# A one-core hybrid layer: another order of block sums, five raw buffers, the residual summed in HBM, transposes by full-width steps and transfers, six pairs by block sums

## The chip, the cores and the metric

The kernel runs on one core of one Trainium2 chip. Its time is device microseconds (us) of one execution, from launch to end. TensorE multiplies matrices and writes into PSUM (eight banks of 128 x 512 fp32); VectorE (DVE), ScalarE (ACT) and GpSimd (POOL) work element by element on SBUF; SyncE (SP) issues most of the transfers between HBM and SBUF, POOL a few.

## The reference

One transformer layer on 256 tokens of 2048 features, all in fp32. `h = rms_norm(x)`; one projection `h @ w_in` gives the inputs of 8 heads of attention (one block of 256 tokens, so the block selection has nothing to choose), of 4 heads of retention, and three gates. Then

```
merged = sigmoid(gate_a) * (oa @ w_o_attn) + sigmoid(gate_r) * (orr @ w_o_ret)
x  = x + merged @ w_out
h2 = rms_norm(x)
g, u = split(h2 @ w_ffn_in, 2)          # 2 x 5632 columns
return x + (silu(g) * u) @ w_ffn_out
```

All weights are read from HBM once, some 300 MB.

## The kernel before

Tokens are two blocks of 128 (`NB`), features are tiles of 128 (`kt`). Each product is `x^T` (features on partitions, stationary) times a weight tile of 128 x 512 (moving), summed over the features in a PSUM bank for each token block. For fp32 precision both operands are split in two fp32r parts, hi and lo, and a product is three matmuls: hi x hi, hi x lo, lo x hi (`mm3`, L97). A weight tile is split by ScalarE (hi, a copy that rounds, L91) and VectorE (lo, a subtraction, L92).

The work is a list of groups. A plain group (`plain`, L130) takes two feature tiles of one block of 512 columns: one split of 128 x 1024 and twelve matmuls. Eight of them make a column block; its evacuation (`ev_...`) follows the last one. The lists stand in the order of the stages: projection, output of attention and retention, `w_out`, then the feed-forward stage. Each turn of the loop at L765 issues loads for up to eight groups ahead (SP, three buffers `raw` of four tiles each), the split of group g, the matmuls of group g - 3, and the jobs due then (`later`, `run_jobs`). A scheduler then orders each engine's instructions by dependency, so neighbours can change places.

The feed-forward stage has eleven pairs j: 512 columns of g and the same of u. The hidden block `silu(g) * u` of each pair must be turned (features on partitions) before it is multiplied by `w_ffn_out`. The pairs come in parts of 3, 3, 3, 2; the output product of a part (`ev_fo`, L719) is done in the next part and added to x1 in SBUF by VectorE (L724), written out at the last part. Pairs in `PLAIN` are two plain column blocks, 192 matmuls. The others go through `strassen` (L183): sums of blocks of the weights (L231, L235, L236, on VectorE) and of x1 (`sum_forms`, made once) give the 2 x 2 blocks in seven products in place of eight: 168 matmuls, and seven more block adds at the evacuation (`ev_gu`, L696). `mixed` deals the groups of block sums evenly among the plain ones.

A turn of a tile (`transposed`, L381): 16 VectorE transposes of 32 partitions x 256 columns, then the hi and lo split. It is used for the query, key and retention inputs, and for the retention output, merged, x1 and hidden tiles (23 of the last four kinds). Buffers: `pair()` (five of 128 x 2 x 512), `unit()` (14 of 128 x 2048), PSUM tags `pm` and `sd` with four banks each.

Of the kernel before, what the change touches and what calls it, by code (L numbers as in the profile page):

```python
# [32 lines left out]
PLAIN = (0, 2, 4, 6, 8, 9)  # L33
# [8 lines left out]
def hybrid_layer_kernel(ctx, tc, xt, x, w_in, w_oa, w_or, w_out, qg, kg, gm, gf, w_fi, w_fo, out):  # L42
# [15 lines left out]

    nc = tc.nc
# [5 lines left out]
    sp = ctx.enter_context(tc.tile_pool(name="sp", bufs=1))  # L65
    att_scope = ExitStack()
# [60 lines left out]
    def rows(w, kts, a, ln):  # L127
        return w[kts[0] * P:(kts[0] + len(kts)) * P, a:a + ln].rearrange("(k p) n -> p k n", p=P)

    def plain(w, cols, kts, lhs, evac, before=None):  # L130
# [6 lines left out]
        def load(i):  # L137
# [38 lines left out]
        while j < len(kts):  # L176

            n = 1 if begin and j < FIRST else SPLIT_KT
            out_groups.append((lambda i=j - j % LOAD_KT: load(i), lambda j=j, n=n: split_(j, n), lambda j=j, n=n: mm(j, n)))
            j += n  # L180
        return out_groups

    def strassen(w, ca, cb, evac):  # L183
# [12 lines left out]
        def first_load(i):  # L196
# [3 lines left out]
            for n in range(2):  # L200
                nc.sync.dma_start(t[:, 2 * n:2 * n + 2, :], rows(w, [k1(4 * i + 2 * n), 0], ca, NC))
# [16 lines left out]
        def load(kk):  # L218
# [3 lines left out]
            for slots, c in ((slice(0, 4, 3), ca), (slice(1, 3), cb)):  # L222
                r = k1(kk) * P
                nc.sync.dma_start(t[:, slots, :], w[r:r + 3 * P, c:c + NC].rearrange("(k p) n -> p k n", p=P)[:, 0:3:2, :])

        def split_(kk, g):
# [154 lines left out]
    def transposed(d, tok, hi, lo, scale=None, sums=None):  # L381
# [192 lines left out]
    def ev_gr(h):  # L574
        def f(pm):
# [9 lines left out]
            transposed(2, y, hi[:, k, :], lo[:, k, :])  # L585
# [13 lines left out]
    def ev_o(n, which):  # L599
        def f(pm):  # L600
# [3 lines left out]
            if which == "r":  # L604
# [7 lines left out]
                transposed(0 if n == 3 else 2, t, hi[:, k, :], lo[:, k, :])  # L612
# [11 lines left out]
    def before_out():  # L624
        for i in range(2):
            x1[i] = unit(F32, (P, NB, 2 * NC))
            nc.sync.dma_start(x1[i], x[:, i * 2 * NC:(i + 1) * 2 * NC].rearrange("(b p) n -> p b n", p=P))

    def x1_cols(n):
        return x1[n // 2][:, :, n % 2 * NC:(n % 2 + 1) * NC]  # L630

    def ev_out(n):
        def f(pm):
            xc = x1_cols(n)
            t = pair()
            for b in range(NB):
                nc.vector.tensor_tensor(xc[:, b, :], pm[b], xc[:, b, :], op=ALU.add)
                nc.scalar.activation(t[:, b, :], xc[:, b, :], AF.Square, accum_out=ss2[:, b, n:n + 1])
            if n % 2 == 0:
                x1T[n // 2] = [unit(shape=(P, 8, S)) for _ in range(2)]  # L640
            hi, lo = x1T[n // 2]
            k = slice(n % 2 * 4, n % 2 * 4 + 4)
            if n % 2 == 0:
                sT[n // 2] = [unit(shape=(P, 2, 4, 2, P)) for _ in range(2)]
            transposed(0 if n == 3 else 2, xc, hi[:, k, :], lo[:, k, :], [g_ffn[:, n * 4 + j:n * 4 + j + 1] for j in range(4)],
                       sums=[t[:, n % 2] for t in sT[n // 2]])
# [23 lines left out]
    extra = []  # L670
# [147 lines left out]
```

## Time and profile before

| | |
|---|---|
| median of three runs | 1587.07 us (1586.04 to 1587.26) |
| the profiled execution | 1589.53 us, its span 1587.8 us |
| granted TensorE clock, mean | 0.988 |
| busy: TensorE, VectorE, ScalarE, POOL | 1540.5, 1244.1, 787.1, 22.8 us |
| matmuls | 6717 |
| transfers | 309.45 MB, 195 GB/s mean |

The span is the time between the first and the last instruction of the profiled execution; about 1.7 us lie around it. A matmul's row is its own duration, pipelined with the next: the step from one to the next is shorter. An engine's idle time matters only where the engine that sets the end waits for it. In the windows below 0 to 757 us reaches to the evacuation of the first column block of the `w_out` product, 828 to 967, 967 to 1190, 1190 to 1384.5 and 1384.5 to 1541 us the four parts of the feed-forward stage (cut at the evacuation of the last hidden block or output column of a part), with the last output product behind them.

### The profile page before, as it was taken

The numbers are of one execution on the slowest core, as the hardware profiler recorded it, in microseconds if no ns is written. First come the engines' busy times: TensorE is split into PE (matmuls) and PEld (weight loads), VectorE is DVE, ScalarE is ACT, GpSimd is POOL, SyncE is SP. The second block draws the span as 40 slices with busy tenths as digits, with TensorE's granted clock in tenths as the row PEclk, the third lists the DMA queues.
The fourth block names the chain that finished last, engine by engine and source line by source line (L and its number), as shares of the span: only waits on it lengthen the run. The fifth ranks groups of instructions, "written<-read, shape, count | busy, mean of one in ns | idle before, by whom it ended". The sixth has DMA issues, their size and how long they took to land.

```text
span 1587.8 us, 17802 instructions
## 1 busy us (share of the span) xinstructions
PE 1540.5 (97%) x6717; PEld 1251.0 (79%) x6717; DVE 1244.1 (78%) x1667; ACT 787.1 (50%) x904; POOL 22.8 (1%) x28
## 2 busy tenths in 40 slices
PE   9999999999999999999999897998999999999998
PEld 6788888888888888888887685676777887877787
DVE  7989877778666565657998979799898878788884
ACT  7465554545553444444465454553554544454442
POOL 1102000000000000000000000000000000000000
PEclk9999999999999999999999998998999999999999
DMA  9455555555565565575555564565666565665563
GB/s 346 161 183 179 174 177 186 185 174 183 178 207 186 189 197 197 186 258 176 198 167 198 180 209 153 192 206 164 209 211 229 192 214 194 205 211 179 194 237 133
DMA packets 163989, 309.45 MB, mean 195 GB/s; under 512 B 6176, under 2 KB 23104, under 8 KB 163648
## 3 DMA queue, kind: packets, MB, share of 16 engines
q1 hardware_dynamic: 163776, 308.31, 58.1%
q8 instruction: 52, 0.85, 0.2%
q14 instruction: 33, 0.27, 0.0%
q0 software_dynamic: 128, 0.02, 0.0%
HBM read 306.20 MB, written 2.10 MB: 194 GB/s over the span
## 4 chain that ended last, share of the span: by engine, by line
PE 64%; DVE 22%; DMA 6%; issue 4%; ACT 3%; SPq 0%; ACTq 0%; DVEq 0%
PE pm L100 20%; PE pm L101 20%; PE pm L99 20%; DVE wlo L92 11%; DVE e L410 6%; DMA raw<-in_w_fi 5%; ACT whi L91 2%; DVE raw L231 1%; PE sd L100 1%; PE sd L101 1%; PE sd L99 1%; DMA raw<-in_w_fo 1%; DVE u L92 1%; DVE raw L235 1%; DVE raw L236 1%
## 5 line engine op out<-in xcount | busy, mean ns | idle before, releaser
L91 ACT ACTIVATE whi<-raw 128x1024 fp32r<-128x1024 f32 (+1 forms) x614 | 637.3, 1054 | 631.8 <-PE pm L101 417.1
L92 DVE TENSOR_TENSOR wlo<-raw,whi 128x1024 fp32r<-128x1024 f32 (+1 forms) x614 | 739.6, 1219 | 268.8 <-ACT whi L91 262.7
L100 PE MATMUL pm<-wlo,u 128*128 128x512 f32 x1912 | 752.8, 394 | 19.4 <-DVE wlo L92 19.2
L99 PE MATMUL pm<-whi,u 128*128 128x512 f32 x1912 | 747.7, 393 | 13.7 <-ACT whi L91 8.1
L101 PE MATMUL pm<-whi,u 128*128 128x512 f32 x1912 | 749.0, 392 | 0.3 <-DVE u L92 0.3
L100 PEld LDWEIGHTS pm<-wlo,u 128*128 128x128 f32 x1912 | 361.6, 189 | 108.3 <-DVE wlo L92 34.1
L99 PEld LDWEIGHTS pm<-whi,u 128*128 128x128 f32 x1912 | 360.7, 189 | 96.6 <-ACT whi L91 15.6
L101 PEld LDWEIGHTS pm<-whi,u 128*128 128x128 f32 x1912 | 361.8, 189 | 75.8 <-DVE u L92 0.7
L410 DVE STREAM_TRANSPOSE e<-e 32x256 f32<-32x256 f32 x432 | 188.3, 436 | 11.0 <-ACT e L520 3.9
L99 PE MATMUL sd<-whi,u 128*128 128x512 f32 x160 | 62.4, 399 | 5.6 <-ACT whi L91 5.6
L100 PE MATMUL sd<-wlo,u 128*128 128x512 f32 x160 | 64.3, 402 | 1.5 <-DVE wlo L92 1.5
L231 DVE TENSOR_TENSOR raw<-raw 128x1024 f32<-128x1024 f32 x40 | 48.9, 1222 | 20.5 <-DMA raw<-in_w_fi 20.4
L101 PE MATMUL sd<-whi,u 128*128 128x512 f32 x160 | 63.5, 397 | 0.0
L91 ACT ACTIVATE u<-e 128x512 fp32r<-128x512 f32 (+1 forms) x56 | 34.5, 654 | 57.3 <-DVE e L410 55.6
L99 PEld LDWEIGHTS sd<-whi,u 128*128 128x128 f32 x160 | 30.3, 191 | 14.7 <-ACT whi L91 8.8
L92 DVE TENSOR_TENSOR u<-e,u 128x512 fp32r<-128x512 f32 (+1 forms) x56 | 39.5, 728 | 0.5 <-ACT u L91 0.5
L100 PE MATMUL pm<-wlo,h 128*128 128x512 f32 x96 | 37.7, 392 | 1.4 <-DVE wlo L92 1.3
L100 PEld LDWEIGHTS sd<-wlo,u 128*128 128x128 f32 x160 | 30.7, 192 | 10.2 <-DVE wlo L92 3.9
L101 PE MATMUL pm<-whi,h 128*128 128x512 f32 x96 | 37.4, 390 | 0.0
L99 PE MATMUL pm<-whi,h 128*128 128x512 f32 x96 | 37.0, 391 | 0.1
L101 PEld LDWEIGHTS sd<-whi,u 128*128 128x128 f32 x160 | 30.8, 192 | 6.3
L410 DVE STREAM_TRANSPOSE e<-u 32x256 f32<-32x256 f32 x64 | 27.9, 436 | 1.3
(142 smaller groups left out, 549.2 us busy)
## 6 DMA issues: line engine op xcount, KB each, us to landing
raw<-in_w_in SPq DMA_DIRECT2D x84, 1024.0 KB, 5.0
raw<-in_w_fi SPq DMA_DIRECT2D x100, 512.0 KB, 4.5
raw<-in_w_fi SPq DMA_DIRECT2D x48, 1024.0 KB, 5.1
raw<-in_w_fo SPq DMA_DIRECT2D x44, 1024.0 KB, 5.1
raw<-in_w_in SPq DMA_DIRECT2D x38, 512.0 KB, 4.3
raw<-in_w_or SPq DMA_DIRECT2D x16, 1024.0 KB, 5.0
raw<-in_w_out SPq DMA_DIRECT2D x16, 1024.0 KB, 5.0
raw<-in_w_oa SPq DMA_DIRECT2D x8, 1024.0 KB, 5.0
```

The source lines that it names most:

```text
L91: nc.scalar.activation(hi, src, AF.Copy)
L92: nc.vector.tensor_tensor(lo, src, hi, op=ALU.subtract)
L99: nc.tensor.matmul(o, lh, rh, start=start, stop=False)
L100: nc.tensor.matmul(o, lh, rl, start=False, stop=False)
L101: nc.tensor.matmul(o, ll, rh, start=False, stop=stop)
L231: nc.vector.tensor_tensor(t[:, 0:2, :], t[:, 0:3:2, :], t[:, 1:2, :].to_broadcast([P, 2, NC]), op=ALU.add)
L235: nc.vector.tensor_tensor(t[:, 0, :], t[:, 0, :], t[:, 2, :], op=ALU.add)
L236: nc.vector.tensor_tensor(t[:, 1, :], t[:, 0, :], t[:, 3, :], op=ALU.add)
L410: nc.vector.transpose(o[:, :, :, q, :], i[:, :, :, f * 32:(f + 1) * 32])
```

## The change

- `PLAIN` loses pair 8: six pairs by block sums, five plain.
- In `split_` the second and third weight sums (L245, L246 after) are made in slots 2 and 3, right behind the first operand's split; before they stood behind the second operand's, in slots 0 and 1.
- In the feed-forward stage five buffers hold raw weights (three `raw`, two `raw2` in the space that attention's constants and two hidden blocks had), and loads are issued 14 groups ahead, not 8.
- 23 tiles are turned by `moved`: two VectorE transposes of 128 partitions x 512 columns (32 x 32 blocks each), four transfers of 32 partitions each into a scratch tile in HBM, one transfer back that puts the 32-blocks in their place. They are issued by POOL, and for the last column of the merged and of the x1 tiles by SP. The hi and lo split then stands four plain groups behind (two for SP's).
- x is loaded by column into `pair()` buffers, x1 is stored to `out` at once, and each output product is copied by ScalarE and added to `out` in HBM by an accumulating transfer from POOL, 32 of 128 x 512.
- The evacuation of a pair by block sums is cut in four steps due at different groups; times of `later` count a plain group as two and a group of block sums as one.

```diff
-PLAIN = (0, 2, 4, 6, 8, 9)
+PLAIN = (0, 2, 4, 6, 9)
...
+        if extra and len(raws) % 5 > 2:
+            raws[key] = extra[0].tile([P, LOAD_KT, NC], F32, tag="raw2", bufs=2, name=nm("raw"))
...
                 split(hi, lo, t[:, 2:4, :])
+                nc.vector.tensor_tensor(t[:, 2, :], t[:, 0, :], t[:, 2, :], op=ALU.add)
+                nc.vector.tensor_tensor(t[:, 3, :], t[:, 2, :], t[:, 3, :], op=ALU.add)
             elif g == 1:
                 split(hi, lo, t[:, 0:2, :])
-                nc.vector.tensor_tensor(t[:, 0, :], t[:, 0, :], t[:, 2, :], op=ALU.add)
-                nc.vector.tensor_tensor(t[:, 1, :], t[:, 0, :], t[:, 3, :], op=ALU.add)
             else:
-                split(hi, lo, t[:, 0:2, :])
+                split(hi, lo, t[:, 2:4, :])
...
+    def moved(d, tok, hi, lo, gains=None, sums=None, tr=None):
+        tr = pair() if tr is None else tr
+        raw = pair().rearrange("p b c -> p (b c)").rearrange("p (q b k t) -> p q b k t", q=4, b=NB, t=32)
+        later(d, moved_rows, tok, tr, raw, nc.gpsimd if d else nc.sync)
+        later(d + 4 if d else 2, moved_split, raw, hi, lo, gains, sums)
+
+    def moved_rows(tok, tr, raw, queue):
...
+        for b in range(NB):
+            nc.vector.transpose(o[:, b], i[:, b])
+        d = dr.tile([4, P, 2 * P], F32, tag="d", bufs=4, name=nm("d"))
+        for q in range(4):
+            queue.dma_start(d[q].rearrange("(g j) x -> j g x", j=32),
+                            tr[q * 32:(q + 1) * 32].rearrange("j (g x) -> j g x", g=4))
+        queue.dma_start(raw.rearrange("p q b k t -> p q (b k t)"), d.rearrange("q p x -> p q x"))
...
     def ev_out(n):
-            xc = x1_cols(n)
+            xc = x1.pop(n)
...
+            nc.sync.dma_start(out[:, n * NC:(n + 1) * NC].rearrange("(b p) n -> p b n", p=P), xc)
...
     def hidden(j, t):
-        if j % 3 == 2:
-            hid[j] = extra[0].tile([P, 2, 4, S], F32R, tag="h", bufs=2, name=nm("h"))
-        else:
-            hid[j] = unit(shape=(P, 2, 4, S))
-        transposed(2, t, hid[j][:, 0], hid[j][:, 1])
+        hid[j] = unit(shape=(P, 2, 4, S))
+        moved(1, t, hid[j][:, 0], hid[j][:, 1])
...
+            step0()
+            later(0.5, step1)
+            later(1, step2)
+            later(2, step3)
...
+    def ev_fo(n):
+        def f(pm):
+            t = pair()
+            for b in range(NB):
+                nc.scalar.activation(t[:, b, :], pm[b], AF.Copy)
+                nc.gpsimd.dma_start(out[b * P:(b + 1) * P, n * NC:(n + 1) * NC], t[:, b, :], accum_op=ALU.add)
...
-        for gg in range(g, min(g + LOAD_AHEAD, NG)):
+        for gg in range(g, min(g + (LOAD_AHEAD if g < n_mix else 14), NG)):
```

VectorE in part 2 before, one weight block of a pair by block sums (`raw_8372`): the first sum, the three operands' `wlo`, the two other sums, and between them a `wlo` of a plain group.

```order
L231 TENSOR_TENSOR raw_8372<-raw_8372 128x1024
L92 TENSOR_TENSOR wlo_8466<-raw_8372,whi_8465 128x1024
L92 TENSOR_TENSOR wlo_8485<-raw_8354,whi_8484 128x1024
L92 TENSOR_TENSOR wlo_8497<-raw_8372,whi_8496 128x1024
L235 TENSOR_TENSOR raw_8372<-raw_8372 128x512
L236 TENSOR_TENSOR raw_8372<-raw_8372 128x512
L92 TENSOR_TENSOR wlo_8520<-raw_8372,whi_8519 128x1024
```

VectorE in part 2 after, from the second sum of one such block (`raw_8169`) to the last operand of the next (`raw_8251`).

```order
L246 TENSOR_TENSOR raw_8169<-raw_8169 128x512
L94 TENSOR_TENSOR wlo_8400<-raw_8169,whi_8399 128x1024
L94 TENSOR_TENSOR wlo_8418<-raw_8169,whi_8417 128x1024
L94 TENSOR_TENSOR wlo_8428<-raw_8239,whi_8427 128x1024
L243 TENSOR_TENSOR raw_8321<-raw_8321 128x1024
L94 TENSOR_TENSOR wlo_8446<-raw_8251,whi_8445 128x1024
L94 TENSOR_TENSOR wlo_8459<-raw_8239,whi_8458 128x1024
L245 TENSOR_TENSOR raw_8251<-raw_8251 128x512
L94 TENSOR_TENSOR wlo_8472<-raw_8251,whi_8471 128x1024
L246 TENSOR_TENSOR raw_8251<-raw_8251 128x512
L94 TENSOR_TENSOR wlo_8488<-raw_8251,whi_8487 128x1024
```

In the order before, the third operand's `wlo` stands right behind the third sum, which its hi part needs. After, the sums have moved ahead of the second operand's `wlo` in the first block; in the second block the third sum still stands right ahead of the third operand.

VectorE in part 2 before, the turn of a plain pair's hidden block (`e_7729` into `e_8006`), to its second split.

```order
L235 TENSOR_TENSOR raw_7904<-raw_7904 128x512
L410 STREAM_TRANSPOSE e_8006<-e_7729 32x2x4x32
L236 TENSOR_TENSOR raw_7904<-raw_7904 128x512
L410 STREAM_TRANSPOSE e_8006<-e_7729 32x2x4x32 x2
L92 TENSOR_TENSOR wlo_8062<-raw_7944,whi_8061 128x1024
L410 STREAM_TRANSPOSE e_8006<-e_7729 32x2x4x32 x4
L92 TENSOR_TENSOR wlo_8076<-raw_7904,whi_8075 128x1024
L410 STREAM_TRANSPOSE e_8006<-e_7729 32x2x4x32 x4
L92 TENSOR_TENSOR wlo_8099<-raw_7944,whi_8098 128x1024
L92 TENSOR_TENSOR u_8005<-e_8006,u_8005 128x512
L92 TENSOR_TENSOR wlo_8113<-raw_7984,whi_8112 128x1024
L92 TENSOR_TENSOR u_8005<-e_8006,u_8005 128x512
```

The turn of the same kind of block after, in the same part (`e_7639` into `e_7915`), from behind its second transpose to the split of the tile that came back (`e_7916`).

```order
L246 TENSOR_TENSOR raw_7724<-raw_7724 128x512
L94 TENSOR_TENSOR wlo_7959<-raw_7724,whi_7958 128x1024
L94 TENSOR_TENSOR wlo_7969<-raw_7769,whi_7968 128x1024
L94 TENSOR_TENSOR wlo_7981<-raw_7724,whi_7980 128x1024
L94 TENSOR_TENSOR wlo_8000<-raw_7769,whi_7999 128x1024
L94 TENSOR_TENSOR wlo_8010<-raw_7810,whi_8009 128x1024
L740 TENSOR_TENSOR e_8039<-sd_7432,e_7423 128x512
L243 TENSOR_TENSOR raw_7893<-raw_7893 128x1024
L94 TENSOR_TENSOR wlo_8030<-raw_7810,whi_8029 128x1024
L739 TENSOR_TENSOR e_7423<-pm_7436,e_7423 128x512
L94 TENSOR_TENSOR wlo_8045<-raw_7839,whi_8044 128x1024
L94 TENSOR_TENSOR u_7914<-e_7916,u_7914 128x4x128 x2
```

The sixteen transposes, five of which stand ahead of the rows shown before, have become two. The split, which followed the last transpose with one `wlo` between, now stands seven `wlo` and four other instructions behind it, and needs a tile that five transfers have moved meanwhile.

POOL's queue after, from the last two column blocks of part 1's output product on: their accumulating stores, then trips of three hidden blocks (four writes into `d`, one read), and the first store of the next part's product.

```order
L772 DMA out<-e_8583 128x512 x2
L772 DMA out<-e_8792 128x512 x2
L416 DMA d_8854<-e_8832 32x4x256 x4
L418 DMA e_8833<-d_8854 128x4x256
L416 DMA d_9426<-e_9389 32x4x256 x4
L418 DMA e_9390<-d_9426 128x4x256
L416 DMA d_9589<-e_9569 32x4x256 x4
L418 DMA e_9570<-d_9589 128x4x256
L772 DMA out<-e_9624 128x512 x2
```

Before, POOL has nothing to do in this stage; its last instruction is one of attention. Now the trips and the stores share its queue, in this order.

## Rows read from the trace of the kernel before

**Rows 1.** The page: busy time, share, instructions; 40 slices, in tenths.

```profile
PE 1540.5 (97%) x6717; PEld 1251.0 (79%) x6717; DVE 1244.1 (78%) x1667; ACT 787.1 (50%) x904; POOL 22.8 (1%) x28
...
DVE  7989877778666565657998979799898878788884
...
PEclk9999999999999999999999998998999999999999
```

**Rows 2.** Windows: engines' busy us (instructions), granted clock, DMA share, GB/s.

```profile
0.00:757.00 757.00, 753.12 (x3380) 622.12 (x3381) 545.26 (x808) 382.41 (x463) 22.82 (x28) 1.00 0.59 197
...
828.00:967.00 139.00, 130.09 (x546) 103.18 (x544) 117.94 (x147) 75.64 (x85) 0.00 (x0) 0.98 0.60 203
967.00:1190.00 223.00, 202.11 (x816) 155.02 (x816) 201.29 (x245) 106.10 (x111) 0.00 (x0) 0.95 0.55 184
1190.00:1384.50 194.50, 191.77 (x841) 157.25 (x842) 157.53 (x185) 95.54 (x97) 0.00 (x0) 1.00 0.61 206
1384.50:1541.00 156.50, 149.74 (x640) 120.11 (x639) 135.70 (x166) 74.48 (x78) 0.00 (x0) 0.99 0.60 202
```

**Rows 3.** Waits 967 to 1190 us: waiter, releaser, us, times, longest.

```profile
PE pm L100 <- DVE wlo L92: 11.6, 11, 2.3
PE sd L99 <- ACT whi L91: 5.4, 5, 3.2
...
DVE wlo L92 <- ACT whi L91: 11.8, 11, 1.2
DVE raw L231 <- DMA raw<-in_w_fi: 6.2, 6, 3.3
```

**Rows 4.** VectorE groups by shape: busy us, mean ns, idle before.

```profile
L92 DVE TENSOR_TENSOR wlo<-raw,whi 128x1024 fp32r<-128x1024 f32 x610 | 736.8, 1222 | 264.2 <-ACT whi L91 258.1
...
L410 DVE STREAM_TRANSPOSE e<-e 32x256 f32<-32x256 f32 x432 | 188.3, 436 | 11.0 <-ACT e L520 3.9
...
L231 DVE TENSOR_TENSOR raw<-raw 128x1024 f32<-128x1024 f32 x40 | 48.9, 1222 | 20.5 <-DMA raw<-in_w_fi 20.4
...
L235 DVE TENSOR_TENSOR raw<-raw 128x512 f32<-128x512 f32 x40 | 27.5, 688 | 0.7
...
L724 DVE TENSOR_TENSOR u<-pm,u 128x512 f32<-128x512 f32 x24 | 15.5, 681 | 0.4 <-PE pm L101 0.4
...
L712 DVE SCALAR_TENSOR_TENSOR e<-e,rstd,e 128x512 f32<-128x512 f32 x10 | 7.0, 743 | 0.0
```

**Rows 5.** The same windows, of the transposes at L410 alone.

```profile
828.00:967.00 139.00, 13.95 (x32) 0.98 0.60 203
967.00:1190.00 223.00, 27.90 (x64) 0.95 0.55 184
1190.00:1384.50 194.50, 20.94 (x48) 1.00 0.61 206
1384.50:1541.00 156.50, 20.91 (x48) 0.99 0.60 202
```

**Rows 6.** Timeline of TensorE, two matmuls twelve apart: start, us.

```profile
1565.79 0.39 PE L99 MATMUL pm<-whi,u 128*128 128x512 f32 x1
...
1568.51 0.39 PE L99 MATMUL pm<-whi,u 128*128 128x512 f32 x1
```

**Rows 7.** Transfers by issuer: count, KB each, median us from issue to landing.

```profile
raw<-in_w_fi SPq DMA_DIRECT2D x100, 512.0 KB, 4.5
...
out<-e SPq DMA_DIRECT2D x8, 256.0 KB, 2.5
...
gqk<-in_qg POOLq DMA_DIRECT2D x1, 0.5 KB, 5.2
```

**Rows 8.** Timeline of POOL: one of its four issues.

```profile
2.03 0.55 POOL L332 DMA_DIRECT2D g_ffn<-in_gf  x1
```

**Rows 9.** Timeline of the end: last matmul, last add.

```profile
1583.24 0.39 PE L101 MATMUL pm<-whi,u 128*128 128x512 f32 x1
...
1583.67 0.69 DVE L724 TENSOR_TENSOR e<-pm,u 128x512 f32<-128x512 f32 x1 [0.67 <-PE pm L101]
```

More of the change, by code (lines that the diff above doesn't have):

```diff
@@ L221, in load @@
             t = raw_tile((ci, "m", kk))
[L222 to L224 removed]
+            k = k1(kk)
+            load_tiles(t, 0, 3, w, [k, k + 2], ca, NC)
+            load_tiles(t, 1, 1, w, [k, k + 2], cb, NC)
         def split_(kk, g):
@@ new lines, in moved_split @@
+    def moved_split(raw, hi, lo, gains, sums):
+        tiles = raw.rearrange("p q b k t -> p b k q t")
+        if gains is not None:
+            for k in range(4):
+                nc.scalar.activation(raw[:, :, :, k], raw[:, :, :, k], AF.Copy, scale=gains[k])
+            f = pair().rearrange("p b (f k s) -> p (b f) k s", f=2, s=P)
+            sum_forms(lambda h, b: tiles[:, b, 2 * h:2 * h + 2], f)
+        for b in range(NB):
+            split(*[x.rearrange("p k (b q t) -> p b k q t", b=NB, t=32)[:, b] for x in (hi, lo)], tiles[:, b])
+        if gains is not None:
+            split(*sums, f)
@@ L405, in transposed_rows, with sum_forms @@
+    def sum_forms(a, f):
+        f = [f[:, i].rearrange("p k (q t) -> p k q t", t=32) for i in range(4)]
+        nc.vector.tensor_tensor(f[0], a(0, 1), a(1, 1), op=ALU.subtract)
+        nc.vector.tensor_tensor(f[2], a(0, 0), a(0, 1), op=ALU.subtract)
+        nc.vector.tensor_tensor(f[1], f[0], a(0, 0), op=ALU.subtract)
+        nc.vector.tensor_tensor(f[3], f[1], a(1, 0), op=ALU.add)
     def transposed_rows(tok, raw, f):
@@ L622, in hybrid_layer_kernel, with load_x_cols, f @@
     x1 = {}
[L624 to L630, printed above, removed]
+    def load_x_cols(n):
+        def f():
+            x1[n] = pair()
+            nc.sync.dma_start(x1[n], x[:, n * NC:(n + 1) * NC].rearrange("(b p) n -> p b n", p=P))
+        return f
     def ev_out(n):
         def f(pm):
-            xc = x1_cols(n)
+            xc = x1.pop(n)
             t = pair()
@@ L638, in f @@
                 nc.scalar.activation(t[:, b, :], xc[:, b, :], AF.Square, accum_out=ss2[:, b, n:n + 1])
+            nc.sync.dma_start(out[:, n * NC:(n + 1) * NC].rearrange("(b p) n -> p b n", p=P), xc)
             if n % 2 == 0:
                 x1T[n // 2] = [unit(shape=(P, 8, S)) for _ in range(2)]
+                sT[n // 2] = [unit(shape=(P, 2, 4, 2, P)) for _ in range(2)]
             hi, lo = x1T[n // 2]
             k = slice(n % 2 * 4, n % 2 * 4 + 4)
[L643 to L646, printed above, removed]
+            moved(0 if n == 3 else 1, xc, hi[:, k, :], lo[:, k, :], [g_ffn[:, n * 4 + j:n * 4 + j + 1] for j in range(4)],
+                  [x[:, n % 2] for x in sT[n // 2]], t)
             if n == 3:
@@ L745, in hybrid_layer_kernel @@
     for n in range(4):
-        groups += plain(w_out, one(n * NC), K, lhs_m, ev_out(n), before=before_out if n == 0 else None)
+        groups += plain(w_out, one(n * NC), K, lhs_m, ev_out(n), before=load_x_cols(n))
     n_mix = len(groups)
@@ L760, in hybrid_layer_kernel @@
         for n in range(4):
-            fo += plain(w_fo, one(n * NC), list(range(4 * j0, 4 * (j0 + p))), lhs_hid, ev_fo(n, j0 + p == NJ))
+            fo += plain(w_fo, one(n * NC), list(range(4 * j0, 4 * (j0 + p))), lhs_hid, ev_fo(n))
         j0 += p
@@ L778, in hybrid_layer_kernel @@
             continue
-        now[0] = m
+        now[0] += groups[m][3]
         if m == n_mix - 8:
@@ L783, in hybrid_layer_kernel @@
         groups[m][2]()
-        run_jobs(m)
+        run_jobs(now[0])
     assert not jobs
```

87 lines of the change are left out of this document (42 added, 45 removed).

## Prediction

> **What bounds the kernel now.** I read the page first, then a table of windows that cuts the span at the stages, then who waited for whom in the worst window, then the groups of instructions by shape, and last the transfers. The page [rows 1] says that TensorE is busy 97% of the span and VectorE 78%; but the row of slices shows VectorE at 8 and 9 tenths from slice 19 on, and the granted clock falling only there. The windows [rows 2] split this. Up to 757 us TensorE is busy 753 of 757 us: nothing done there for VectorE can pay. In the feed-forward stage, parts 1 to 4 (828 to 1541 us) take 139, 223, 194.5 and 156.5 us.
>
> To see what TensorE alone would need, I take its undisturbed step from two matmuls twelve apart in the plain tail [rows 6]: 1568.51 - 1565.79 = 2.72 us for 12, 0.2267 us each. Times the matmuls of each window: part 1 has 546 x 0.2267 = 123.8 us, part 2 816 -> 185.0, part 3 841 -> 190.6, part 4 640 -> 145.1. So the parts lose 15.2, 38.0, 3.9 and 11.4 us, 68.5 us together. VectorE's busy time over the same TensorE need is 0.95, 1.09, 0.83 and 0.94: the loss follows this ratio, and in part 2 VectorE has more work than TensorE. The waits of part 2 [rows 3] say the same: TensorE waits for `wlo` (VectorE) and `whi`, VectorE for ScalarE (11.8 us) and for weights (6.2 us). The granted clock of 0.95 there is the two-level clock at 1.2 GHz for a tenth of that window; every stretch of it follows such stalls, so it goes with them.
>
> **The change, part by part.**
> *Transposes.* A 512-column tile takes 16 instructions of 0.436 us [rows 4] now, 7.0 us; after, two over all 128 partitions and 512 columns. No row shows that shape. Bounds: one half-size instruction, 0.44, and two of them, 0.87. From VectorE's 512 and 1024 column rows (0.688 and 1.222) a column costs 1.05 ns and an instruction 0.15 us; 256 columns give 0.42, near the 0.436 seen, so 512 give 0.69. I take 0.70. A tile saves 7.0 - 1.4 = 5.6 us of VectorE. The windows of parts 1 to 4 hold 32, 64, 48 and 48 of these instructions [rows 5], so 2, 4, 3 and 3 tiles.
> *Residual.* The 32 adds at L724 (0.68 us) leave VectorE; ScalarE makes 32 copies of the same shape, and ScalarE is at 106 of 223 us in part 2 [rows 2], so they are hidden. 24 of them fall in parts 2 to 4 [rows 4], 8 each, 5.5 us.
> *Sixth pair of block sums.* TensorE: 192 - 168 = 24 matmuls, 24 x 0.2267 = -5.4 us, in part 3. VectorE: 12 more `wlo` (12 x 1.22 = 14.6), 8 x (1.22 + 2 x 0.69) = 20.8, and seven adds and two products against two products (7 x 0.68 = 4.8): +40.2 us.
> *VectorE after*, busy: part 1 117.9 - 11.2 = 106.7; part 2 201.3 - 22.4 - 5.5 = 173.4; part 3 157.5 - 16.8 - 5.5 + 40.2 = 175.4; part 4 135.7 - 16.8 - 5.5 = 113.4. Over TensorE's need (123.8, 185.0, 185.2, 145.1) that is 0.86, 0.94, 0.95 and 0.78. TensorE now has the longer work in every part.
> *Order of the sums, and five buffers.* ScalarE makes its half of the third operand only when the third sum (L236) is done, and VectorE's `wlo` of it waits for that. In the order before, the `wlo` stands right behind the third sum; in the order after, the first of the two blocks shown has another `wlo` between, the second has none. So I let the 11.8 us of VectorE waiting for ScalarE in part 2 fall by half. VectorE's wait for weights at L231, 20.5 us in the run [rows 4], should go: the loads stand 14 groups ahead in five buffers. The short steps of the pair's evacuation break up a run of nine VectorE instructions in which no `wlo` was made.
> *What is left of the stalls.* The loss goes with the ratio: 2% at 0.83 (part 3), 8% at 0.94 (part 4), 12% at 0.95 (part 1). After: part 1 at 0.86 about 3.5%, 4.3 us, and 2 us for the first round trip on SP's queue, 130; parts 2 and 3 at 0.94 and 0.95 would lose 8%, 15 us; as the waits for ScalarE and weights fall I halve it, 7 us: 192 each; part 4 at 0.78 loses 1.5%: 147. Sum 661 against 713: **-52 us**.
> *The way round HBM.* Each of 23 tiles now takes four writes and a read that waits for them; 21 of these trips are on POOL's queue (the last feature tile of two stages goes on SP's). While POOL's read waits for its four writes, the accumulating stores and the next trip stand behind it; nobody waits for the stores but the buffers of `pair`. The price of a trip: POOL issues take 0.55 us [rows 8], so 2.2 for four; a 256 KB store from SP landed in 2.5 us, a 512 KB load in 4.5 [rows 7]: 2.2 + 2.5 + 0.55 + 4.5 = 9.8 us. The upper bound takes POOL's own slow landings, 5.2 us [rows 7], for both legs: 13.2 us. What covers it is VectorE's work between the transposes and the split that needs the tile: the order of VectorE after, above, shows one trip of part 2: from the second transpose to the split seven `wlo` and one other full-width instruction and three half-width ones, 8 x 1.22 + 3 x 0.69 = 11.8 us by [rows 4]; the ten trips ahead of the last one have 11 to 15. At 9.8 nothing waits; at 13.2 some six trips wait 1 to 2 us, 10 us together. Nearest in kind is the first (large transfers), so I take it as hidden. Traffic: 24 MB (23 x 2 x 0.52) and 8 MB more on 309 MB, at 0.55 to 0.61 busy [rows 2]: hidden. The Trainium skill, "DMA: Bandwidth & Descriptors", section on the anatomy of a DMA on the gpsimd path, gives about 2.0 us plus bytes over 436 GB/s; worked out, 2.2 + 3.2 + 0.55 + 3.2 = 9.2 us, an estimate by that page, near the lower of my bounds; no run here has yet shown a large transfer on that queue.
> *Loads of x by column, stores of x1 on SP.* Four small loads and four stores in SP's order; a store holds the loads behind it until the column ends, but these belong to groups ten or more ahead (27 us). Nothing, with at most 1 us each where a buffer is short, 4 us.
> *End.* Now: last matmul at 1583.24, add at 1583.67 (0.69), store 2.5 us [rows 7, 9]. After: a ScalarE copy, then an accumulating store from POOL; between 0 (a copy as long as the add, the same landing) and +2.7 (the 5.2 us landing). I take +1.
> *Sum* for the profiled execution: 1589.5 - 52 + 1 = 1538.5. That execution stands 2.5 us above the median of 1587.07, so **1536 us**.
>
> **The rivals.**
> *All the stalls go.* VectorE below TensorE in every part, buffers three groups deep: then the loss of 68.5 and 5.4 us go, 1587 - 73.9 + 1 = 1514 us. For it: part 3, at 0.83, loses only 2%. Against: at 0.94 part 4 lost 8%, and parts 2 and 3 stand there.
> *The stalls stay as they are for their ratio, and the trips wait.* Without the halving, 8 us more in parts 2 and 3 each, and 10 us for trips at 13.2: 1536 + 16 + 10 = 1562. For it: pairs of buffers are five in number and a tile now holds three of them for a whole trip; the sixth pair buys 5.4 us of TensorE with 40.2 us of VectorE.
> *Slower than before: trips on POOL's queue.* VectorE's split of a tile stands in its order whether the tile is there or not; each us over the cover of some 12 is lost in every feed-forward trip that has no slack, about ten. The gain of 51 is eaten at 51 / 10 = 5 us over it, a trip of 17 us. At 20 us: 1536 + 10 x 8 = 1616. For it: a trip moves 1024 rows of 1 KB, 512 out and 512 back, and the one issue that I have [rows 8] is of 128 rows, while VectorE was idle; 0.55 us need not hold for these. Against: at that price a trip of 17 us needs transfers far slower than any of [rows 7], the slow one included: (17 - 2.75) / 2 = 7.1 us a leg. The Trainium skill, "SBUF — State Buffer", section on the two sides, says that such descriptors cannot be written while VectorE runs a one-input fp32 copy in its two-port mode, 620 ns becoming 3100; in the feed-forward stage only the transposes have one input, and by that rule applied to every issue a trip would be five times 2.5 us longer, 22 us, 1636; no run here shows it.
> *The change does nothing:* VectorE is not what TensorE waits for. It would give 1587 - 5 = 1582, by the 24 matmuls alone; the waits of [rows 3] exclude it.
>
> **How the numbers follow.** Forecast 1536 with its own range 1522 to 1552: 55%. All stalls gone, 1505 to 1522: 20%. Stalls and trips, 1552 to 1584: 16%. Within 0.2% (3 us, about what a measurement of this kernel tells from no change): 2%. Slower: 7%. So faster 0.91, same 0.02, slower 0.07. A range of 1510 to 1568 holds the forecast's 55, some 16 of the 20 below it and 9 of the 16 above: 8 in 10.
>
> **What would show it.** Right: part 2 (between the first and second half of the feed-forward stage's block sums) near 192 us, VectorE's busy total near 1244 - 129 - 22 + 40 = 1133 us, transposes near 0.70 us, hardly any wait of VectorE for weights, a granted clock near 1.0 throughout, 6693 matmuls. The slower rival shows as VectorE or ScalarE waiting for a transfer into `e`, with POOL's issues far over 0.55 us. All gone shows as TensorE's waits in that stage under 10 us. The forecast is wrong if the four writes and the read together take over 15 us, or if full-width transposes cost near 2 us.

## The result, and the profile after

The changed kernel takes 1560.68 us (median of four, 1560.40 to 1564.28) against 1587.05 before: ratio 0.984, interval 0.9823 to 0.9857. It is faster, inside the wide range of 1510 to 1568 but outside the forecast's own 1522 to 1552: the gain is 26 us where 51 were forecast. Where the other 25 went is the question below. Some 3 of them belong to no stage: the forecast took 2.5 us off because the profiled execution before stood above its median, and the one after stands 0.3 below (1560.42). The stages have to answer for 22.

The page of the changed kernel: engines' busy time, VectorE's 40 slices and the granted clock, as in [rows 1].

```profile
PE 1521.7 (98%) x6693; PEld 1244.5 (80%) x6693; DVE 1126.0 (72%) x1356; ACT 821.0 (53%) x949; POOL 113.4 (7%) x165
...
DVE  7989867576655555545575788898889888878762
...
PEclk9999999999999999999999999999999999999999
```

VectorE lost 118 us of work, about as forecast (1126 us are left for 1133), and the matmuls are the 6693 expected. So the work was counted rightly; the time is in waits. Windows at the same stages as [rows 2] (cut at the end of the first column of `w_out`, the end of `w_out` and the ends of parts 1 to 4); columns as there:

```profile
0.00:760.00 760.00, 756.57 (x3400) 625.20 (x3401) 501.11 (x696) 384.02 (x464) 44.37 (x63) 1.00 0.62 208
760.00:834.00 74.00, 70.67 (x300) 56.67 (x299) 45.25 (x57) 38.59 (x59) 8.83 (x15) 0.98 0.74 256
834.00:971.00 137.00, 129.34 (x551) 104.82 (x550) 109.51 (x121) 78.59 (x85) 2.94 (x5) 0.98 0.65 219
971.00:1169.00 198.00, 189.94 (x816) 153.10 (x815) 172.61 (x182) 111.63 (x120) 18.68 (x28) 0.99 0.76 243
1169.00:1360.00 191.00, 188.00 (x817) 152.10 (x816) 168.32 (x176) 111.38 (x118) 15.78 (x23) 1.00 0.76 247
1360.00:1496.00 136.00, 133.88 (x584) 108.84 (x583) 107.09 (x110) 72.35 (x77) 11.67 (x18) 1.00 0.74 244
1496.00:1558.70 62.70, 53.30 (x236) 43.81 (x234) 22.14 (x19) 24.40 (x31) 11.10 (x13) 0.95 0.58 133
```

Before, the last three columns of `w_out` lost nothing (313 x 0.2267 = 71.0):

```profile
757.00:828.00 71.00, 71.00 (x313) 58.32 (x313) 65.07 (x102) 39.98 (x59) 0.00 (x0) 1.00 0.54 177
```

With the same step of 0.2267 us per matmul, each window's length less its matmuls gives its loss. Beside it what the prediction left there, and what the experiment k_late_split below has in its own windows. The end before is 1541 to 1587.8 us with 189 matmuls. The cuts between `w_out` and part 1 do not fall at the same matmul (300 in the window after, 271 in that of k_late_split), so the sum of these two rows is firmer than each:

| stage | before | forecast | after | k_late_split |
|---|---|---|---|---|
| last three columns of `w_out` | 0 | 0 | 6.0 | 0 |
| part 1 | 15.2 | 6.2 | 12.1 | 6.6 |
| part 2 | 38.0 | 7.0 | 13.0 | 7.2 |
| part 3 | 3.9 | 7.0 | 5.8 | 2.6 |
| part 4 | 11.4 | 1.9 | 3.6 | 1.5 |
| the end | 4.0 | 5 | 9.2 | 9.7 |

The shortfall is no single stage: 6 us each at the end of `w_out`, in part 1 and in part 2, and 4 at the end. The waits of the changed kernel from 760 to 1496 us say what the first three have in common (waiter, releaser, us, times, longest):

```profile
DVE raw L243 <- DMA raw<-in_w_fi: 38.8, 22, 4.7
ACT u L93 <- DMA e<-d: 20.4, 9, 6.5
...
ACT e L424 <- DMA e<-d: 18.6, 3, 8.2
DVE e L436 <- ACT e L424: 17.6, 3, 7.9
...
PE pm L102 <- DVE wlo L94: 10.9, 11, 3.6
PE sd L102 <- DVE wlo L94: 6.7, 6, 3.7
```

ScalarE waits 39 us for tiles that come back from HBM (`e<-d`), VectorE behind it, and TensorE behind both. One such trip, the second x1 tile, first on POOL, then on ScalarE, in two views of the timeline (start, us, and the idle time before with its releaser):

```profile
788.28 2.19 POOL L416 DMA_DIRECT2D d<-e  x4 [13.60 <-ACT whi L93]
796.52 0.76 POOL L418 DMA_DIRECT2D e<-d  x1 [6.05 <-DMA d<-e]
```

```profile
794.43 1.06 ACT L93 ACTIVATE whi<-raw 128x1024 fp32r<-128x1024 f32 x1 [1.66 <-PE pm L103]
803.68 1.71 ACT L424 ACTIVATE e<-e,g_ffn 128x256 f32<-128x256 f32 x4 [8.19 <-DMA e<-d]
```

From the first write's issue to the landing are 15.4 us (803.68 - 788.28). ScalarE was done at 795.5, stood 8.2 us before the tile's gain (L424), and only then made the next weight part that TensorE needed. VectorE had ended the second transpose at 787.7, worked on weights, and then stood 7.9 us before the tile's first sum (L436):

```profile
787.02 0.70 DVE L413 STREAM_TRANSPOSE e<-e 128x512 f32<-128x512 f32 x1
...
804.62 0.43 DVE L436 TENSOR_TENSOR e<-e 128x256 f32<-128x256 f32 x1 [7.87 <-ACT e L424]
```

The price of trips, in the transfers of 750 to 1560 us (count, KB, median us to landing):

```profile
raw<-in_w_fi SPq DMA_DIRECT2D x118, 512.0 KB, 4.6
...
out<-e POOLq DMA_DIRECT2D x32, 256.0 KB, 6.3
d<-e POOLq DMA_DIRECT2D x56, 128.0 KB, 4.5
e<-d POOLq DMA_DIRECT2D x14, 512.0 KB, 6.5
...
d<-e SPq DMA_DIRECT2D x4, 128.0 KB, 5.7
e<-d SPq DMA_DIRECT2D x1, 512.0 KB, 5.0
```

In the 14 trips on POOL's queue the read (L418) is issued 5.5 to 9.1 us after the first write, 7.4 in the mean; with the landing of 6.5 a trip takes 13.9 us. The last two rows are the trip of the last x1 tile, on SP's queue.

### The profile page after: what moved, and what is told of

Read it like the earlier page. It is cut to its first block, busy times and chain, and to the rows that moved or that the text cites. A ratio compares the mean times of both kernels' runs of the same rounds, so it can differ in the third digit from the quotient of the medians.

```text
span 1558.7 us, 17843 instructions
## 1 busy us (share of the span) xinstructions
PE 1521.7 (98%) x6693; PEld 1244.5 (80%) x6693; DVE 1126.0 (72%) x1356; ACT 821.0 (53%) x949; POOL 113.4 (7%) x165
## 5 line engine op out<-in xcount | busy, mean ns | idle before, releaser
L94 DVE TENSOR_TENSOR wlo<-raw,whi 128x1024 fp32r<-128x1024 f32 (+1 forms) x626 | 752.5, 1218 | 307.4 <-ACT whi L93 302.9
L93 ACT ACTIVATE whi<-raw 128x1024 fp32r<-128x1024 f32 (+1 forms) x626 | 654.2, 1056 | 599.8 <-PE pm L103 488.9
L102 PE MATMUL pm<-wlo,u 128*128 128x512 f32 x1968 | 770.8, 392 | 12.2 <-DVE wlo L94 11.9
L101 PE MATMUL pm<-whi,u 128*128 128x512 f32 x1968 | 769.0, 391 | 4.3 <-ACT whi L93 2.9
L103 PE MATMUL pm<-whi,u 128*128 128x512 f32 x1968 | 767.6, 390 | 0.0
L101 PEld LDWEIGHTS pm<-whi,u 128*128 128x128 f32 x1968 | 370.9, 189 | 86.1 <-ACT whi L93 5.7
L103 PEld LDWEIGHTS pm<-whi,u 128*128 128x128 f32 x1968 | 370.7, 188 | 76.8 <-DVE u L97 0.4
L416 POOL DMA_DIRECT2D d<-e x84 | 46.2, 557 | 976.0 <-DVE e L413 960.5
L243 DVE TENSOR_TENSOR raw<-raw 128x1024 f32<-128x1024 f32 x48 | 58.7, 1222 | 38.8 <-DMA raw<-in_w_fi 38.8
L101 PE MATMUL sd<-whi,u 128*128 128x512 f32 x192 | 74.7, 392 | 2.8 <-ACT whi L93 2.8
L103 PE MATMUL sd<-whi,u 128*128 128x512 f32 x192 | 75.6, 394 | 0.0
L445 DVE STREAM_TRANSPOSE e<-e 32x256 f32<-32x256 f32 x128 | 55.8, 436 | 6.1 <-ACT e L555 4.1
L101 PEld LDWEIGHTS sd<-whi,u 128*128 128x128 f32 x192 | 36.0, 188 | 11.9 <-ACT whi L93 4.5
L772 POOL DMA_DIRECT2D out<-e x32 | 27.6, 902 | 229.2 <-ACT e L771 227.6
L245 DVE TENSOR_TENSOR raw<-raw 128x512 f32<-128x512 f32 x48 | 33.0, 687 | 0.7
L246 DVE TENSOR_TENSOR raw<-raw 128x512 f32<-128x512 f32 x48 | 32.9, 685 | 0.4
```

The source lines that it names most:

```text
L93: nc.scalar.activation(hi, src, AF.Copy)
L94: nc.vector.tensor_tensor(lo, src, hi, op=ALU.subtract)
L101: nc.tensor.matmul(o, lh, rh, start=start, stop=False)
L102: nc.tensor.matmul(o, lh, rl, start=False, stop=False)
L103: nc.tensor.matmul(o, ll, rh, start=False, stop=stop)
L245: nc.vector.tensor_tensor(t[:, 2, :], t[:, 0, :], t[:, 2, :], op=ALU.add)
```

## The experiments

Fifteen kernels, each timed beside the kernel before on its own chip. The ratio to before, not the median, is compared between rows; the changed kernel has 0.984 (0.9823 to 0.9857). 0.001 is 1.6 us.

| kernel | median us | ratio | interval |
|---|---|---|---|
| a_longer_cover | 1558.6 | 0.9818 | 0.9795 to 0.9842 |
| b_sp_queue | 1556.7 | 0.9804 | 0.9790 to 0.9817 |
| c_x1_vector | 1550.5 | 0.9763 | 0.9750 to 0.9777 |
| e_plain_tail | 1557.7 | 0.9809 | 0.9795 to 0.9822 |
| k_late_split | 1540.0 | 0.9697 | 0.9684 to 0.9709 |
| d_all_vector | 1573.0 | 0.9903 | 0.9889 to 0.9917 |
| f_five_pairs | 1563.1 | 0.9847 | 0.9828 to 0.9865 |
| g_three_buffers | 1586.9 | 0.9990 | 0.9977 to 1.0004 |
| m_late_five_pairs | 1544.5 | 0.9732 | 0.9713 to 0.9751 |
| n_late_old_sums | 1538.9 | 0.9695 | 0.9678 to 0.9712 |
| o_vector_three_buffers | 1599.4 | 1.0077 | 1.0062 to 1.0093 |
| p_best | 1535.5 | 0.9671 | 0.9652 to 0.9690 |
| q_late_tail | 1534.9 | 0.9682 | 0.9663 to 0.9701 |
| s_late_x1 | 1548.0 | 0.9763 | 0.9748 to 0.9778 |
| t_late_hidden | 1552.5 | 0.9778 | 0.9756 to 0.9799 |

**a_longer_cover.**

```diff
-        later(d + 4 if d else 2, moved_split, raw, hi, lo, gains, sums)
+        later(d + 6 if d else 2, moved_split, raw, hi, lo, gains, sums)
```

> Only the distance changes: the split of a tile that went through HBM is due six plain groups behind its transposes, not four (POOL's trips only), some 5.4 us more cover. Theory 1 (a trip takes 13 to 16 us, not 9.8, and ScalarE and VectorE stand in their order before the split until it lands): the three waits of 3 to 8 us for the x1 tiles in the w_out stage and those for hidden tiles go, about 6 us before 834 us and 3 to 6 us in parts 1 and 2, so 1549 to 1553 us; ScalarE's waits for a transfer into e (18.6 and 25.0 us in the changed kernel) fall under 10 us together. Theory 2 (the trips' traffic slows the loads of weights, and that is the loss): time stays within 1558 to 1563, VectorE's wait for w_fi stays near 38 us and TensorE's waits stay. Theory 3 (buffers of pair() are short): slower, 1563 to 1575, since a tile holds its buffers 5 us longer.

The interval overlaps the changed kernel's, and ScalarE still waits 13.4 us at L424 and 25.0 for the other tiles. That is no evidence against theory 1, since the edit did not do what it says: in the order of instructions L424 of the x1 tiles stands where it stood, six `whi` behind the evacuation, one ahead of the next. The scheduler that turns the code into queues chose the same place for it; later code alone did not hold it back.

**b_sp_queue.** SP's queue in the changed kernel around the last x1 tile: 12 us without an issue, until the store of x1 may go; loads behind it; the last tile's four writes cut in two by three loads; the read 13 us after the first write.

```profile
822.96 0.37 SPq L139 DMA_DIRECT2D raw<-in_w_fi  x1
835.16 0.38 SPq L672 DMA_DIRECT2D out<-e  x1
837.46 0.88 SPq L139 DMA_DIRECT2D raw<-in_w_fi  x2
838.82 0.33 SPq L416 DMA_DIRECT2D d<-e  x1
841.02 4.10 SPq L139 DMA_DIRECT2D raw<-in_w_fi  x3
845.17 1.45 SPq L416 DMA_DIRECT2D d<-e  x3
...
851.90 0.38 SPq L418 DMA_DIRECT2D e<-d  x1
```

```diff
-        later(d, moved_rows, tok, tr, raw, nc.gpsimd if d else nc.sync)
+        later(d, moved_rows, tok, tr, raw, nc.gpsimd)
...
-            nc.sync.dma_start(out[:, n * NC:(n + 1) * NC].rearrange("(b p) n -> p b n", p=P), xc)
+            nc.gpsimd.dma_start(out[:, n * NC:(n + 1) * NC].rearrange("(b p) n -> p b n", p=P), xc)
```

> Two things leave SP's queue for POOL's: the stores of x1 to out (four of 512 KB) and the last column's trip of merged and x1. Theory 1 (loads of w_fi stand behind the last store until the column ends, and the last trip's writes stand behind three loads, 19 us in all): the loss after the last evacuation of w_out (12.1 us between 834 and 971 us in the changed kernel) falls by 5 to 8 us, 1553 to 1556 us. Theory 2 (the queue's order does nothing, the trip is long by itself): within 1559 to 1563. Theory 3: the stores now stand ahead of the trips on POOL's queue and make them later: 1563 to 1568.

The ratio is lower by 0.0036, 6 us, but a_longer_cover, nearly the changed kernel and on the same chip, is lower by 0.0022 and overlaps it. In the trace the second gate's evacuation, after the boundary, stands at 928.4 us against 930.2; but in a_longer_cover, where SP's queue is as in the changed kernel, it stands at 927.1. So no gain from SP's queue is shown.

**c_x1_vector.** `moved(...)` of the x1 tiles is replaced by the `transposed(...)` with sums of the kernel before.

> The four x1 tiles are turned by 16 VectorE steps each again, as in the kernel before; all else as in the changed kernel. Theory 1 (the loss around the end of w_out is these four trips): of the 18.1 us lost between 760 and 971 us 8 to 12 go, though VectorE gets 4 x 5.6 = 22 us more there: 1549 to 1553 us. Theory 2 (the loss there is the traffic of x, x1 and weights on SP): 1558 to 1562. Theory 3 (VectorE's work in that stage decides): 1563 to 1568.

12 us faster than the changed kernel: 22 us more of VectorE's work bought 12 us, and no x1 tile has a trip to wait for. The run also takes four trips out of the traffic; k_late_split keeps them. Over the whole run TensorE's waits for `wlo` into `pm` fall from 11.9 to 6.4 us, those for `sd`, in the parts, stay (6.7 and 7.2).

**e_plain_tail.** For the last two columns, a load when the product begins, and its evacuation:

```diff
+            last[n] = pair()
+            nc.gpsimd.dma_start(last[n], out[:, n * NC:(n + 1) * NC].rearrange("(b p) n -> p b n", p=P))
...
+                    nc.vector.tensor_tensor(t[:, b, :], pm[b], t[:, b, :], op=ALU.add)
+                    nc.sync.dma_start(out[b * P:(b + 1) * P, n * NC:(n + 1) * NC], t[:, b, :])
```

> In the last part the last two columns of the output are not added by an accumulating transfer: out's column is loaded into SBUF by POOL when the column's product begins, VectorE adds it to the product, SP stores it. Theory 1 (the chain copy on ScalarE, issue 0.84 and landing 6.3 us on POOL is what the end grew by): the end falls by 3 to 5 us, 1556 to 1558 us, and the last add stands some 4 us before the span's end, against 9 now. Theory 2 (the end is set by the loads of w_fo and the splits before it): 1559.5 to 1562.

The last steps of the changed kernel, and of this one:

```profile
1549.34 0.60 ACT L771 ACTIVATE e<-pm 128x512 f32<-128x512 f32 x1 [0.76 <-PE pm L103]
1550.23 0.84 POOL L772 DMA_DIRECT2D out<-e  x1 [0.51 <-ACT e L771]
```

```profile
1549.48 0.69 DVE L780 TENSOR_TENSOR e<-pm,e 128x512 f32<-128x512 f32 x1 [0.67 <-PE pm L103]
```

The last step starts at the same time in both, but the span ends 9.4 us after it (1558.7) there and 4.2 us (1553.7) here; before it was 4.1 [rows 9]. So the accumulating store on POOL's queue costs 5 us at the end against a plain one on SP's; queue and adding were changed together, so which of them costs it is not shown. The times agree (5 us by the ratio), though the interval ends only 0.0001 below that of the changed kernel.

**k_late_split.** The edit that a_longer_cover meant; `late`, the plain groups by which a split stands behind its transposes, is nine, for the last two hidden tiles four. Each gain at L424 and the first sum of an x1 tile, and the splits of all other tiles, are held behind what is written before them:

```diff
-        later(d + 4 if d else 2, moved_split, raw, hi, lo, gains, sums)
+        later(d + late if d else 2, moved_split, raw, hi, lo, gains, sums)
...
+                r = nc.scalar.activation(raw[:, :, :, k], raw[:, :, :, k], AF.Copy, scale=gains[k])
+                tc.keep_in_program_order(r)
```

> The run before, a_longer_cover, left the place of the x1 splits in the order of ScalarE and VectorE as it was: the scheduler moved them forward again. Here the first instructions of each split are held in the order in which they are written, nine plain groups behind the transposes (four for the last hidden tile), so that in the w_out stage they stand behind the next column's evacuation. Theory 1 (what is lost is the two engines standing before a split whose tile is still on its way round HBM, 15 us): ScalarE's wait for L424's tile falls from 18.6 to under 6 us, for the hidden tiles from 25 to under 12, and the time is 1546 to 1552. Theory 2 (traffic): 1557 to 1562. Theory 3 (a tile holds its pair() buffers longer and stops the next tile): over 1562.

1540.0 us, 21 less than the changed kernel and below theory 1's range, with every trip, transfer and tile still there. ScalarE now passes the place without a stop, and the trip is as long as ever (POOL, then ScalarE, for the same tile):

```profile
783.67 2.19 POOL L416 DMA_DIRECT2D d<-e  x4 [7.32 <-ACT whi L93]
793.03 0.76 POOL L418 DMA_DIRECT2D e<-d  x1 [7.16 <-DMA d<-e]
```

```profile
804.02 1.06 ACT L93 ACTIVATE whi<-raw 128x1024 fp32r<-128x1024 f32 x1 [0.42 <-ACT e L677]
804.99 1.69 ACT L424 ACTIVATE e<-e,g_ffn 128x256 f32<-128x256 f32 x4
```

The read is issued 9.4 us after the first write, even later than before; but L424 now stands behind the next column's evacuation (L677), 21.3 us after the first write, without a wait. Its waits, 760 to 1475 us, against those above (39.0 us for `e<-d`, 2.6 now):

```profile
ACT u L430 <- DMA e<-d: 2.6, 2, 2.3
PE pm L102 <- DVE wlo L94: 2.5, 3, 0.9
...
PE sd L102 <- DVE wlo L94: 1.2, 2, 0.6
```

Three of its windows, `w_out`, part 2 and the end (the column of the table above is from these and the three between, 0.2267 us per matmul):

```profile
762.00:823.00 61.00, 61.00 (x271) 50.53 (x270) 43.69 (x51) 35.13 (x49) 8.85 (x15) 1.00 0.88 301
...
962.00:1154.00 192.00, 186.99 (x815) 151.90 (x814) 172.20 (x181) 112.48 (x120) 18.74 (x28) 1.00 0.78 252
...
1475.00:1537.70 62.70, 53.00 (x234) 43.54 (x232) 21.87 (x19) 24.11 (x30) 10.94 (x13) 0.96 0.58 131
```

The first of them moves 301 GB/s at 0.88 of the DMA engines and TensorE loses nothing: traffic, theory 2, is excluded as the cause.

**s_late_x1 and t_late_hidden.** `late` for the x1 tiles alone, and for all others alone.

> Late, held splits for the x1 tiles alone; the others held in the order written, but four groups behind, as in the changed kernel. Theory 1 (the changed kernel's loss beside the forecast is two thirds the boundary, as c_x1_vector gave 12 us, and a third hidden tiles): 1547 to 1550. Theory 2 (most is the hidden tiles, and c_x1_vector gained by lifting traffic): 1554 to 1560.

> The opposite: late, held splits for the hidden, merged and retention tiles, the x1 tiles held but four groups behind. Theory 1: the hidden tiles' third, 1550 to 1554. Theory 2: 1541 to 1547. With s_late_x1 it shows whether the 21 us of k_late_split are the sum of both places.

12 and 10 us below the changed kernel by the ratios; together 22, and k_late_split has 23. The two places add up, and each run keeps just the other wait, though the tiles there are held in the written order too: being late is what takes the wait away, not being held. s_late_x1 first, then t_late_hidden.

```profile
ACT u L430 <- DMA e<-d: 19.5, 8, 5.9
```

```profile
ACT e L424 <- DMA e<-d: 19.5, 3, 8.5
```

**d_all_vector.** All 23 tiles by `transposed(...)`.

> All 23 tiles are turned on VectorE by 16 steps again; sum order, buffers, residual in HBM, six pairs stay. Theory 1 (the way round HBM buys VectorE 129 us, and that is what part 2 and 3 need; its price is the boundary of w_out alone): parts 2 and 3 get VectorE above TensorE again (196 and 192 us of work for 185), so 1570 to 1590. Theory 2 (the gain of 26 us comes from the other parts of the change, buffers and sum order, and the turns only cost trips): 1550 to 1560.

By the ratios the way round HBM is worth 10 us as built and 33 with late splits. The window of part 2:

```profile
975.00:1180.00 205.00, 193.22 (x809) 154.30 (x810) 190.46 (x226) 111.73 (x120) 7.01 (x8) 0.97 0.67 216
```

VectorE's work over TensorE's need (809 x 0.2267) is 1.04 there, 190.46 / 183.4, and the loss 21.6 us: the loss follows the ratio, as the prediction read it from [rows 2].

**g_three_buffers and o_vector_three_buffers.** Three raw buffers and `LOAD_AHEAD` everywhere; in the second with all turns on VectorE too.

```diff
-        if extra and len(raws) % 5 > 2:
+        if False:
...
-        for gg in range(g, min(g + (LOAD_AHEAD if g < n_mix else 14), NG)):
+        for gg in range(g, min(g + LOAD_AHEAD, NG)):
```

> Three raw buffers and loads eight groups ahead in the feed-forward stage, as before the change. VectorE's wait for w_fi did not go with five buffers, it rose from 20.5 to 38.8 us. Theory 1 (that wait is of an engine that has time now, the buffers still hide the longer landings of 6.5 us): 1568 to 1580 without them. Theory 2 (the buffers do nothing): 1559 to 1562. Theory 3 (loads issued 14 groups ahead crowd the trips): 1552 to 1557.

> d_all_vector (no trips, 1573.0 us) with three raw buffers and loads eight groups ahead. g_three_buffers showed 26 us for the buffers beside the trips. Theory 1 (the trips' traffic makes the loads land late, 6.5 for 5.1 us, and the buffers only pay for that): 1573 to 1579 here. Theory 2 (block sums want 1 MB each 4.1 us whatever else moves, three buffers are short by themselves, and more so with six pairs): 1588 to 1600.

The buffers are worth 24 us by the ratios with the trips, more than any theory of the first run had, and 28 without; theory 2 of the second holds, and o_vector_three_buffers is slower than the kernel before. The wait that they take away is one the prediction never looked at (g_three_buffers, from 760 us to the end):

```profile
ACT whi L93 <- DMA raw<-in_w_fi: 120.8, 56, 7.5
...
ACT whi L93 <- DMA raw<-in_w_fo: 48.3, 18, 6.5
```

It stood in the trace of the kernel before as well, over the whole run:

```profile
ACT whi L91 <- DMA raw<-in_w_fi: 85.4, 38, 6.3
```

ScalarE's wait for raw weights goes with five buffers; VectorE's at L243 doesn't (36.3 us in g_three_buffers, 38.8 in the changed kernel). Nothing shows that one to cost time: k_late_split has 27.8 us of it, n_late_old_sums 14.1, and their times are the same.

**f_five_pairs and m_late_five_pairs.** `PLAIN = (0, 2, 4, 6, 8, 9)`, on the changed kernel and on k_late_split.

> The sixth pair goes back to plain: 24 matmuls more (5.4 us of TensorE), 40 us less of VectorE. Theory 1 (TensorE bounds part 3, the pair is worth its matmuls): 1565 to 1567 us. Theory 2 (VectorE's work and the extra trip-laden stretch take it back): 1558 to 1563.

> On k_late_split (1540.0 us): the sixth pair back to plain. With no engine standing before a trip, theory 1 (the pair is worth its 24 matmuls, and in f_five_pairs stalls hid that) gives 1544 to 1547; theory 2 (VectorE's 40 us more in part 3 take it back in any case) 1538 to 1541.

In the changed kernel the sixth pair can't be told from nothing (0.984 and 0.9847). In k_late_split it gives 0.0035, 5.6 us (4.5 by the medians): the 24 matmuls of 5.4 us.

**n_late_old_sums.** L245 and L246 back behind the second operand, in slots 0 and 1, on k_late_split.

> On k_late_split: the second and third weight sums back in their old place behind the second operand's split. Theory 1 (ScalarE waits for them there, and VectorE for ScalarE; some 2 to 3.5 us in each of parts 2 and 3): 1544 to 1550. Theory 2 (with VectorE below TensorE in every part the order is hidden): 1538 to 1541.

No difference, and here is one row to learn from: in this run ScalarE waits far longer for the third sum (39.4 us in k_late_split, 62.1 in the changed kernel), and it costs nothing.

```profile
ACT whi L93 <- DVE raw L248: 130.8, 43, 6.1
```

**p_best and q_late_tail.** k_late_split with the end of e_plain_tail; p_best also with x1 on VectorE.

> k_late_split with the x1 tiles on VectorE (c_x1_vector) and the last two columns summed by VectorE (e_plain_tail). Theory 1 (three losses in three places, each with its own cause: the first product after the boundary ends 9 us earlier in c_x1_vector than in k_late_split, 849 for 858, and the end is 4 us shorter): 1540 - 9 - 4 = 1527, 1524 to 1531. Theory 2 (x1's 22 us on VectorE come out later as stalls): 1535 to 1541.

> k_late_split with the last two columns summed by VectorE and stored by SP, x1 still by way of HBM. In p_best the x1 tiles on VectorE added nothing to the late splits: the second evacuation of the feed-forward stage stands at 862.6 us there and at 862.9 in k_late_split, and p_best came out at 1535.5 where 1527 was expected. Theory 1 (x1 on VectorE and late splits cure the same loss, the end is a separate one of 5 us): 1534 to 1537. Theory 2 (the four microseconds of p_best came from x1 on VectorE, the end gives nothing): 1538 to 1541.

Both are near 1535 us, the fastest kernels here, 25 us under the changed one; they can't be told apart, so x1 on VectorE and late splits cure one loss, not two, and the expectation of 1527 was wrong. The end of q_late_tail (last add at 1528.64, span 1533.1) is 4.5 us, as in e_plain_tail, against 9.7 in k_late_split. The intervals of the two overlap, so this gain of about 5 us is shown by the trace, not by the times.

## Why the prediction was wrong

*What held.* The transposes took 0.691 us (forecast 0.70), VectorE's total was within 7 us, the sixth pair is worth its matmuls once nothing hides it, and the losses that were left over for parts 1, 2 and 4 (6.2, 7 and 2 us) are what k_late_split has (6.6, 7.2, 1.5). With its trips covered the change takes 1540 us, 4 from the forecast; that it comes so near is in part luck, since part 3 lost 4 us less than forecast and the end 5 more.

```profile
L413 DVE STREAM_TRANSPOSE e<-e 128x512 f32<-128x512 f32 x46 | 30.4, 691 | 0.0
```

*The step that failed: "the way round HBM".* The prediction took 9.8 us for a trip, between 9.8 and 13.2, "as hidden" under a cover of 11 to 15. Measured: 13.9 in the mean, 11.3 to 17.9 one by one. Both legs were mis-sized, not the issues: POOL's write landed in 4.5 us (2.5 taken, from SP), its read in 6.5 (4.5 taken), and the read waited on to 7.4 us where 4.7 was reckoned.

For the hidden tiles the cover was right and the price alone failed. From the second transpose to the place where ScalarE stood, the ten of them in the feed-forward stage that it waited for had 10.3 to 12.5 us. One of part 2, whose second transpose ended at 974.2:

```profile
974.53 2.18 POOL L416 DMA_DIRECT2D d<-e  x4 [63.17 <-DVE e L413]
...
990.17 1.15 ACT L93 ACTIVATE u<-e 128x512 fp32r<-128x512 f32 x2 [3.73 <-DMA e<-d]
```

ScalarE stood from 986.4: 12.2 us of cover, 15.6 of trip. The bound that the prediction set aside, 13.2 us with 10 us lost, was nearly right here: the hidden and other tiles cost 10 (t_late_hidden). For the four x1 tiles at the end of `w_out` no cover was worked out; one of them was given 2 us. The second of them, shown above, had 7.8 us (787.7 to 795.5) for its 15.4, the third 8.1 for 14.7. They cost 12 (s_late_x1).

Why the legs were longer stays open. POOL's queue alone is not the reason, since the one x1 trip on SP's queue had 5.7 and 5.0. The trips ran beside weight loads, at 0.65 to 0.76 of the DMA engines in the windows above; seven trips before 700 us, at 0.63, had 3.9 and 4.9. That traffic lengthened them is argued from this, not shown.

The second rival named the time, 1562, and half the reason: the trips did wait. Its other half, that stalls stay as they are for their ratio (15 us in part 2 and in part 3), is refuted by k_late_split with 7.2 and 2.6.

By the Trainium skill, "DMA: Bandwidth & Descriptors", section on the anatomy of one DMA on the gpsimd path, the estimate was 9.2 us; the trace has 13.9, so the measurement decides. The rule of the Trainium skill, "SBUF — State Buffer", section on the two sides, by which a trip would have come to 22 us, was not put to the test: POOL's 84 issues of writes took 0.557 us in the mean, as its issue before [rows 8], and none of them ran beside a transpose.

*The end.* Forecast +1, with 2.7 as the upper end; it is +5 (4.1 to 9.4 us after the last step). The landing of the small transfer [rows 7] was no bound for an accumulating one: 6.3 us and an issue of 0.84. With the 12 and the 10 us above, this makes up the shortfall, as far as intervals of 2 to 3 us on each side can tell.

*Loads by column and stores on SP.* Nothing was forecast, 4 us at most, and b_sp_queue shows no gain that a_longer_cover, with SP's queue unchanged, doesn't show as well within their intervals.

*Order of the sums, and buffers.* The prediction halved the loss of parts 2 and 3 for both. The order is worth nothing (n_late_old_sums). The buffers are worth 24 to 28 us, but not by the wait that was named: VectorE's wait at L243 was to go and rose from 20.5 to 38.8. So neither reason for the halving held; that part 2 in k_late_split loses just the 7 us left for it is luck. What the buffers gave was ScalarE's wait.

## What to carry to other kernels

A transfer that a queue must wait for is hidden only by the time between its last producer and the place of its first user in that queue. Look for the first engine that stands there, at every place where such a transfer is made and not in one stage alone, and price the transfer by rows of its own kind, or by the upper bound where there are none. Where a scheduler sets that place, writing the user later may change nothing: read the order, hold the instruction, and check that the wait is gone in the trace. A wait that grows on an engine with time to spare need not be a loss (130.8 us at L248, and the same time), so undo a part before crediting or blaming it.

## What the runs showed that was not expected

A 512 KB read on POOL's queue landed in 6.5 us where weights of that size on SP's took 4.6, and a 128 KB write in 4.5; the accumulating 256 KB store took 6.3, where a plain one of that size on SP's took 2.5 before [rows 7]. Three raw buffers, as in the kernel before, cost 24 us beside six pairs by block sums. The granted clock follows the stalls: 0.95 in part 2 before [rows 2], 0.99 in the changed kernel and 1.00 in k_late_split.
